# Weight casts behind the copies, matmuls on a constant at the start, and first weights loaded in two parts, in a two-layer encoder

## The chip, the cores and the metric

The kernel runs on one core of a Trainium2 chip. The metric is the device time of one execution in microseconds (us). The kernel before the change took 2218.75, 2219.17 and 2223.41 us in three runs; the median is 2219.17.

Five engines work side by side, each with its own queue of instructions that it takes in order: TensorE (PE), VectorE (DVE), ScalarE (ACT), GpSimd (POOL) and SyncE (SP). They wait for each other through semaphores. The loads are issued by SP; the transfers that add to what is already there are issued by POOL.

## The reference, cut to what matters

Two layers over 528 tokens (16 learned ones and 512 of the input) of 1024 channels, all in fp32. Each layer is a half-weighted SwiGLU feed-forward network (FFN), a mixer (gated linear attention and softmax attention, merged) and a second FFN.

```
def swiglu(x, w_gate, w_up, w_down):
    return (jax.nn.silu(x @ w_gate) * (x @ w_up)) @ w_down
...
    for l in range(DEPTH):
        h = h + 0.5 * swiglu(rmsnorm(h, norm_gains[l, 0]),
                             ffn_w_gate[l, 0], ffn_w_up[l, 0], ffn_w_down[l, 0])
        h = h + mixer(rmsnorm(h, norm_gains[l, 1]), w_in[l], ...)
        h = h + 0.5 * swiglu(rmsnorm(h, norm_gains[l, 2]),
                             ffn_w_gate[l, 1], ffn_w_up[l, 1], ffn_w_down[l, 1])
    return rmsnorm(h, final_norm)[:, N_META:]
```

The inner width of an FFN is 2816. The change touches only the four FFNs and the start of the first.

## The kernel before, in words

**Operands in two parts.** Every fp32 operand is split into a rounded part (hi, type fp32r) and the remainder (lo). A product of two operands is three matmuls, hi with hi, hi with lo and lo with hi. For a weight of 128x1024 the hi part is made by ACT in a cast (L244, about 1.05 us, into one of 4 buffers `whi`) and the remainder by DVE in a subtraction (L245, about 1.22 us, into one of 4 buffers `wlo`).

**Pairs and products.** The columns of gate and up are worked on in 11 pairs of 128-column blocks, in groups of 4, 4 and 3. For one pair the 2x2 block product with seven multiplications (Strassen and Winograd) is used: products 1, 2, 5, 6, 7, 4 and 3, each with its own combination of the weights and of the normed input. In this text (p,n) is product n of pair p, counted from pair 0 of its FFN. A product is 24 matmuls of 128x128 with 128x264 (L618) and needs one weight of 128x1024 in its hi and lo parts. In program order pair p+1's products 1 and 2 stand around pair p's 7 and 4. In the very first FFN, pair 0 is computed without the seven-product form, in two plain products (L575) with two weights each, so that TensorE can begin before all of the input is there; then come (1,1), (1,2), (1,6), (1,5), (2,1), (1,7), (2,2), (1,4), (1,3), (2,6), (2,5), (3,1).

**Weights.** SP loads a weight into one of three raw buffers. Four of the seven weights of a pair are sums and differences of blocks: `sums` (called from L250) has ACT negate a block (L192, tile `s`), and POOL issue transfers that add a block from memory or another tile to it (L197, `s<-win`, `w<-s`, `w<-win`, `s<-w`). One pass makes s3 and s2 for products 7 and 6, the other s1 and s4 for products 5 and 3. `use(j)` is called when product j is written out, and makes casts up to three or four products ahead.

**Banks.** A pair's products add up in three PSUM areas X, Y and Z. (p,6), (p,7) and (p,4) continue in X, where (p,1) began. ACT copies X out after products 1, 6 and 7 (`snapshot`, L629, tile `snap`), and the matmuls of the next product into that area wait for the copy. Y is freed by DVE's add of product 2 (L636), which reads the copy of product 1.

**What sets the order.** Instructions are written in one sequence, and a scheduler puts them on the engines by priorities; `tc.high_priority()` pulls an instruction forward, and `tc.issue_after(ins)` (through `after`) keeps one from being placed ahead of `ins`. Once placed, an engine's queue is fixed: an instruction that waits holds up all behind it. In the kernel before, the copies have ordinary priority, and one cast alone, that of the first FFN's (1,6), is held behind an instruction: `W.behind`, the last copy of the first two plain products (L584).

Of the kernel before, what the change touches and what calls it, by code (L numbers as in the profile page):

```python
# [17 lines left out]
P = 128  # L18
# [25 lines left out]
HELD = 4  # L44
SQUARES = {(1, "2"): (0, 1), (1, "6"): (2, 3), (1, "5"): (4, 5), (2, "1"): (6, 7)}
# [115 lines left out]

class Weights:
# [3 lines left out]
    def __init__(self, nc, after, raw, hi, lo, wts, win):  # L166
        self.nc, self.raw, self.hi_pool, self.lo_pool, self.wts, self.win = nc, raw, hi, lo, wts, win
        self.long = self.short = None
        self.loads = []
        for t, col in zip(PLAN, COLUMN):  # L170
            if t[0] == "op":
                self.loads.append(t[1:])
            elif col % SLAB == 0:
                self.loads.append(col // SLAB)
        self.at = {load: i for i, load in enumerate(self.loads)}
        self.made, self.fetched, self.got, self.summed, self.raws = 0, 0, {}, {}, {}
        self.pos, self.behind, self.after = 0, None, after
# [4 lines left out]
    def block(self, f, i, name, pool=None, tag="raw"):  # L182

        w = (pool or self.raw).tile([P, SLAB], F32, tag=tag, name=f"w{name}_{f[0]}{f[1]}_{i}")
        first = f + (i, name) == (0, 0, 0, "11")
        for a in np.split(np.arange(SLAB), 2 if first else 1):
            self.nc.sync.dma_start(w[:, a[0] : a[-1] + 1], self.dram(f, i, name)[:, a[0] : a[-1] + 1])
        return w

# [40 lines left out]
    def make(self, upto):  # L230
        nc = self.nc
        while self.made < min(upto, len(self.loads)):
# [8 lines left out]
            for a in np.split(np.arange(SLAB), 2 if s == 0 else 1):  # L241
                cs = slice(a[0], a[-1] + 1)
                with self.after(self.behind if load == ((0, 0), 1, "6") else None):
                    nc.scalar.copy(hi[:, cs], w[:, cs])  # L244
                nc.vector.tensor_tensor(lo[:, cs], w[:, cs], hi[:, cs].bitcast(F32), ALU.subtract)  # L245
# [6 lines left out]
    def use(self, j):  # L252
        self.make(j + AHEAD_MADE - (j < AHEAD_MADE))
# [25 lines left out]
def build(tc, ctx, xt, wts, win, par, w2, const, umask, out):  # L279
# [75 lines left out]
    S.activation(whole, eps.broadcast_to([P, P]), AF.Copy, scale=0.0, bias=1.0)  # L355
    b64, diag2 = ct[:, C_B64 : C_B64 + P], ct[:, C_DIAG : C_DIAG + P]
# [202 lines left out]
    def ffn(l, f, norm, done, following):  # L559
# [62 lines left out]
        def finished(p, product):  # L622
# [3 lines left out]
            def snapshot(name):  # L626
                t = slots["snap"].tile([P, T], F32, tag="snap", name=nm("snap"))[:, :n]
                st[name] = v2(t)
                S.copy(st[name], acc)  # L629
# [583 lines left out]
    bp = [block_pools()]  # L1213
    nc.sync.dma_start(h(1), xt[:, 1])
    first.whole(0)
# [89 lines left out]
```

## Time and profile before

| what | us |
|---|---|
| runs | 2218.75, 2219.17, 2223.41 (median 2219.17) |
| the profiled execution | 2222.56 |
| its span, first to last instruction | 2220.7 |
| TensorE (PE) busy | 2193.3 |
| VectorE (DVE) busy | 1515.2 |
| ScalarE (ACT) busy | 1218.6 |
| GpSimd (POOL) busy | 150.5 |
| first matmul starts | 6.59 |

All times in the profile count from the span's start. The four FFNs lie at about 6 to 385 us, 766 to 1100, 1129 to 1500 and 1866 to 2210; the mixers lie between. A row of a timeline gives the start, the length, the engine, the line, the operation, what is written and read, and a count, and in brackets the idle time ahead of it and what ended it. A row of the chain of waits gives start, length and what the end of the program hung on at that time. In the rows of windows the granted TensorE clock is 1.00 at full speed and 0.50 at half.

### The profile page before, as it was taken

What the parts mean: (1) busy time and instruction counts of PE and PEld (TensorE: products, weight loads), DVE (VectorE), ACT (ScalarE), POOL (GpSimd) and SP (SyncE); (2) the same over time, 40 slices, a digit from 0 to 9 for tenths busy, and PEclk for the clock granted to TensorE, in tenths of its full rate; (3) what the DMA queues carried; (4) which work ended last, traced back from release to release, by engine and by line L of the source; (5) the groups of instructions that cost most, each with busy time, mean ns of one, the idle gap of its engine ahead of it and who ended that gap; (6) DMA issues with size and microseconds to landing.
All of it is one profiled execution on the core that took longest, in us unless ns stands there. A gap on an engine that the chain in (4) does not pass through costs nothing.

```text
span 2220.7 us, 39865 instructions
## 1 busy us (share of the span) xinstructions
PE 2193.3 (99%) x16538; PEld 2094.3 (94%) x16538; DVE 1515.2 (68%) x2406; ACT 1218.6 (55%) x1824; POOL 150.5 (7%) x176
## 2 busy tenths in 40 slices
PE   8999999999999999999999999999999999999998
PEld 8999999999999999999999999999888888989897
DVE  7757567577876676565786575675889767756575
ACT  8535355455784574443575363554557837636354
POOL 1011000000000010101010110000000001101010
PEclk9999999999999999999999999999999999999999
DMA  8669563212113585867677685632211146968562
GB/s 258 182 175 231 142 152 110 77 48 68 48 39 126 140 218 143 202 171 176 170 174 191 171 215 142 157 110 77 67 67 48 48 133 158 240 152 223 152 168 67
DMA packets 87542, 312.85 MB, mean 141 GB/s; under 512 B 9664, under 2 KB 11840, under 8 KB 87360
## 3 DMA queue, kind: packets, MB, share of 16 engines
q1 hardware_dynamic: 60816, 217.67, 28.9%
q0 software_dynamic: 24768, 90.19, 22.9%
q8 instruction: 130, 2.13, 0.4%
q10 hardware_dynamic: 1776, 2.43, 0.4%
q14 instruction: 52, 0.43, 0.1%
HBM read 263.07 MB, written 2.10 MB: 119 GB/s over the span
## 4 chain that ended last, share of the span: by engine, by line
PE 88%; DVE 5%; ACT 4%; DMA 2%; issue 1%; DVEq 0%; SPq 0%; ACTq 0%; POOLq 0%
PE ss L618 38%; PE ss L409 26%; PE mm L409 13%; PE sm L409 2%; DVE wlo L245 1%; PE sm L1004 1%; DMA w<-win 1%; ACT whi L244 1%; PE ss L979 1%; ACT t L392 1%; PE sm L1020 1%; PE ss L980 1%; PE sm L1021 1%; PE ss L600 1%; PE ss L1190 0%
## 5 line engine op out<-in xcount | busy, mean ns | idle before, releaser
L618 PE MATMUL ss<-xc,whi 128*128 128x264 f32 (+1 forms) x4720 | 862.2, 284 | 4.3 <-ACT snap L629 4.1
L618 PEld LDWEIGHTS ss<-xc,whi 128*128 128x128 f32 x4720 | 732.7, 189 | 6.4 <-ACT snap L629 5.3
L618 PE MATMUL ss<-xc,wlo 128*128 128x264 f32 (+1 forms) x2360 | 670.0, 284 | 1.0 <-DVE wlo L245 1.0
L409 PE MATMUL ss<-g,whi 128*128 128x264 f32 (+1 forms) x2620 | 482.5, 300 | 0.0
L618 PEld LDWEIGHTS ss<-xc,wlo 128*128 128x128 f32 x2360 | 445.5, 189 | 1.6 <-DVE wlo L245 1.6
L409 PEld LDWEIGHTS ss<-g,whi 128*128 128x128 f32 x2620 | 380.8, 188 | 15.9
L409 PE MATMUL mm<-x,whi 128*128 128x264 f32 (+1 forms) x1712 | 384.3, 314 | 0.0
L244 ACT CAST whi<-w 128x1024 fp32r<-128x1024 f32 (+1 forms) x220 | 229.9, 1046 | 248.5 <-PE ss L409 113.4
L244 ACT CAST whi<-raw 128x1024 fp32r<-128x1024 f32 x190 | 199.2, 1048 | 278.3 <-PE ss L618 91.5
L245 DVE TENSOR_TENSOR wlo<-w,whi 128x1024 fp32r<-128x1024 f32 (+1 forms) x220 | 266.7, 1217 | 105.8 <-ACT whi L244 104.4
L409 PE MATMUL ss<-g,wlo 128*128 128x264 f32 (+1 forms) x1310 | 302.4, 300 | 0.0
L245 DVE TENSOR_TENSOR wlo<-raw,whi 128x1024 fp32r<-128x1024 f32 x190 | 232.0, 1221 | 93.9 <-ACT whi L244 89.8
L409 PEld LDWEIGHTS mm<-x,whi 128*128 128x128 f32 x1712 | 279.1, 188 | 15.9 <-DVE x L398 0.2
L409 PE MATMUL mm<-x,wlo 128*128 128x264 f32 (+1 forms) x856 | 265.3, 315 | 0.0
L409 PEld LDWEIGHTS ss<-g,wlo 128*128 128x128 f32 x1310 | 209.4, 188 | 8.1
L245 DVE TENSOR_TENSOR wlo<-s,whi 128x1024 fp32r<-128x1024 f32 x86 | 105.1, 1222 | 93.5 <-ACT whi L244 93.5
L244 ACT CAST whi<-s 128x1024 fp32r<-128x1024 f32 x86 | 90.3, 1051 | 142.6 <-PE ss L618 122.7
L409 PEld LDWEIGHTS mm<-x,wlo 128*128 128x128 f32 x856 | 159.6, 188 | 8.3
L192 ACT ACTIVATE s<-w 128x1024 f32<-128x1024 f32 x86 | 91.2, 1060 | 84.8 <-DMA w<-win 54.5
L546 DVE SCALAR_TENSOR_TENSOR t<-ss,rs 128x528 f32<-128x528 f32 (+1 forms) x64 | 44.3, 700 | 126.1 <-PE ss L409 126.0
L197 POOL DMA_DIRECT2D w<-win x43 | 37.7, 876 | 958.6 <-DVE wlo L245 396.7
L197 POOL DMA_DIRECT2D s<-win x43 | 39.9, 927 | 536.9 <-ACT s L192 536.9
(284 smaller groups left out, 2838.0 us busy)
## 6 DMA issues: line engine op xcount, KB each, us to landing
w<-win SPq DMA_DIRECT2D x218, 512.0 KB, 4.8
raw<-wts SPq DMA_DIRECT2D x190, 512.0 KB, 3.3
s<-win POOLq DMA_DIRECT2D x43, 512.0 KB, 7.0
w<-win POOLq DMA_DIRECT2D x43, 512.0 KB, 7.9
w<-s POOLq DMA_DIRECT2D x43, 512.0 KB, 5.4
s<-w POOLq DMA_DIRECT2D x43, 512.0 KB, 6.7
h<-xt SPq DMA_DIRECT2D x3, 528.0 KB, 6.9
out<-h SPq DMA_DIRECT2D x2, 512.0 KB, 2.9
```

What stands on the lines that cost most here:

```text
L192: self.nc.scalar.activation(t, w, AF.Copy, scale=-1.0)
L197: self.nc.gpsimd.dma_start(t, src, accum_op=ALU.add)
L244: nc.scalar.copy(hi[:, cs], w[:, cs])
L245: nc.vector.tensor_tensor(lo[:, cs], w[:, cs], hi[:, cs].bitcast(F32), ALU.subtract)
L392: prev_act[0] = S.activation(*args, **kw).ins
L409: TE.matmul(acc.half[i][:width], lhs, rhs[:, acc.spans[i]], start=first, stop=last)
L546: V.scalar_tensor_tensor(cut(dst[rows]), pv[rows], -0.5 * f, cut(rs[rows]), ALU.mult, ALU.mult)
L600: TE.matmul(acc[:, j], a[:, j, k], b[:, at], start=k == 0 and i == 0, stop=k == last and i == 2)
L618: TE.matmul(acc[:, j], a[:, j, k], b[:, at], start=bool(begin and k == 0 and i == 0), stop=k == len(x) - 1 and i == 2, skip_group_check=no ...
L979: TE.matmul(s[:n, i, :HF], lhs, kh[:, hs], start=True, stop=False)
L980: TE.matmul(s[:n, i, :HF], lhs, kl[:, hs], start=False, stop=True)
L1004: TE.transpose(tp[:, j * w + u * n : j * w + (u + 1) * n], pr[:n, (2 * c2 + j) * P : (2 * c2 + j + 1) * P], ident[:n, :n])
```

## The change

1. **Matmuls on a constant.** DVE fills a 128x512 tile with a constant, and TensorE runs ten matmuls on it into PSUM that nobody reads, ahead of the first product.
2. **First weights in two parts.** The first two weights ("11" and "12" of pair 0) are loaded in two parts: first the columns of the first of four row blocks (256 of 1024), later the rest (`finish_loads`). Their casts and remainders are made in the same two parts. SP's queue at the start is now: input chunk 0, head of "11", input chunk 1, head of "12", rest of "11", rest of "12", the other input chunks. Before: input chunks 0 and 1, "11" in two halves, "12", the other chunks.
3. **Casts behind the copies.** Each copy that frees a bank (`snapshot`) gets high priority and is stored in `W.behind`, and every FFN weight cast for gate and up is issued after the copy that was stored last when it is written.
4. **When casts are made.** `use(j)` makes casts up to j + 4 for j above 4, and up to 6 for the first five; before it was j + 3 below 4 and j + 4 from there on. The casts of (1,6) and (1,5) are so written at the use of (1,2) and not of (1,1).

```
+WARMING = 10
...
+PIECES = (slice(0, 1), slice(1, KC // 2))
+def by_pair(ap):
+    return ap.rearrange("p (w k m) -> p w k m", w=2, k=KC // 2)
...
     def block(self, f, i, name, pool=None, tag="raw"):
         w = (pool or self.raw).tile([P, SLAB], F32, tag=tag, name=f"w{name}_{f[0]}{f[1]}_{i}")
-        first = f + (i, name) == (0, 0, 0, "11")
-        for a in np.split(np.arange(SLAB), 2 if first else 1):
-            self.nc.sync.dma_start(w[:, a[0] : a[-1] + 1], self.dram(f, i, name)[:, a[0] : a[-1] + 1])
+        src = self.dram(f, i, name)
+        if f + (i,) == (0, 0, 0) and name in ("11", "12"):
+            head, tail = [(by_pair(w)[:, :, ks], by_pair(src)[:, :, ks]) for ks in PIECES]
+            self.nc.sync.dma_start(*head)
+            self.rest.append(tail)
+        else:
+            self.nc.sync.dma_start(w, src)
         return w
+    def finish_loads(self):
+        for t in self.rest:
+            self.nc.sync.dma_start(*t)
...
-            for a in np.split(np.arange(SLAB), 2 if s == 0 else 1):
-                cs = slice(a[0], a[-1] + 1)
-                with self.after(self.behind if load == ((0, 0), 1, "6") else None):
-                    nc.scalar.copy(hi[:, cs], w[:, cs])
-                nc.vector.tensor_tensor(lo[:, cs], w[:, cs], hi[:, cs].bitcast(F32), ALU.subtract)
+            for part in [[by_pair(t)[:, :, ks] for t in (hi, lo, w)] for ks in PIECES] if s < 2 else [(hi, lo, w)]:
+                with self.after(None if isinstance(load, int) else self.behind):
+                    nc.scalar.copy(part[0], part[2])
+                nc.vector.tensor_tensor(part[1], part[2], part[0].bitcast(F32), ALU.subtract)
...
     def use(self, j):
-        self.make(j + AHEAD_MADE - (j < AHEAD_MADE))
+        self.make(j + AHEAD_MADE if j > AHEAD_MADE else AHEAD_MADE + 2)
...
+    idle = slot("t", F32R)[:, :512]
+    V.tensor_copy(idle, eps.broadcast_to([P, 512]))
+    for _ in range(WARMING):
+        TE.matmul(pair()[:, 0], idle[:, :P], idle, start=True, stop=True)
...
             def snapshot(name):
                 t = slots["snap"].tile([P, T], F32, tag="snap", name=nm("snap"))[:, :n]
                 st[name] = v2(t)
-                S.copy(st[name], acc)
+                with tc.high_priority():
+                    W.behind = S.copy(st[name], acc).ins
...
+    W.fetch(1)
     nc.sync.dma_start(h(1), xt[:, 1])
+    W.fetch(2)
+    W.finish_loads()
     first.whole(0)
```

Three places show what moves on the engines. The lines of the change are numbered differently from those of before: L260 is the cast (L244 before), L261 the remainder (L245), L650 the copy (L629), L209 the negation (L192), L657 DVE's add of product 2 (L636), L638 the product's matmuls (L618), L440 the matmuls of the norm's totals (L420). Tile numbers differ too.

**ACT at the end of (1,2) in the first FFN**, before. whi_484 and whi_488 are the hi parts for (1,6) and (1,5), snap_516 is the copy of (1,1), t are squares for the norm.

```order
L455 ACTIVATE t_518<-h 128x528
L584 COPY c_378<-ss_382 128x528
L244 CAST whi_484<-w_00_1_220 128x1024
L244 CAST whi_488<-w_00_1_249 128x1024
L455 ACTIVATE t_520<-h 128x528
L629 COPY snap_516<-ss_483 128x528
L244 CAST whi_524<-w_00_2_383 128x1024
L455 ACTIVATE t_562<-h 128x528
```

And with the change (snap_533 is the copy, whi_541, whi_545 and whi_549 the three casts):

```order
L475 ACTIVATE t_587<-h 128x528
L475 ACTIVATE t_590<-h 128x528
L650 COPY snap_533<-ss_508 128x528
L260 CAST whi_541<-w_00_1_245 128x1024
L260 CAST whi_545<-w_00_1_274 128x1024
L260 CAST whi_549<-w_00_2_408 128x1024
L260 CAST whi_593<-s_00_1_242 128x1024
L475 ACTIVATE t_625<-h 128x528
```

The copy has moved from behind two casts to the front of them, and a third and a fourth cast follow directly. On DVE the three remainders wlo_542, wlo_546 and wlo_550 now stand in a row ahead of the add c_585 of (1,2):

```order
L261 TENSOR_TENSOR wlo_542<-w_00_1_245,whi_541 128x1024
L261 TENSOR_TENSOR wlo_546<-w_00_1_274,whi_545 128x1024
L261 TENSOR_TENSOR wlo_550<-w_00_2_408,whi_549 128x1024
L657 TENSOR_TENSOR c_585<-snap_533,ss_540 128x2x264
L261 TENSOR_TENSOR wlo_594<-s_00_1_242,whi_593 128x1024
```

Before, DVE had two remainders, an addition of squares, the third remainder and then this add. Earlier on ACT, the negation of pair 1's block 11 stood ahead of both copies of the first product (L584); now it stands behind the first of them and one activation.

**ACT from (2,1) to (1,4) in the first FFN**, before. snap_676 is the copy of (2,1), snap_706 that of (1,7), s_00_3_814 the negation for pair 3.

```order
L244 CAST whi_648<-w_00_1_572 128x1024
L415 CAST t_710<-t_518 128x528
L244 CAST whi_678<-s_00_1_252 128x1024
L629 COPY snap_676<-ss_647 128x528
L192 ACTIVATE s_00_3_814<-w_00_3_745 128x1024
L629 COPY snap_706<-ss_483 128x528
```

And with the change (snap_701 of (2,1), snap_731 of (1,7)):

```order
L260 CAST whi_673<-w_00_1_597 128x1024
L650 COPY snap_701<-ss_672 128x528
L260 CAST whi_703<-s_00_1_277 128x1024
L435 CAST t_735<-t_535 128x528
L209 ACTIVATE s_00_3_839<-w_00_3_770 128x1024
L650 COPY snap_731<-ss_508 128x528
```

The copy of (2,1) has changed places with the cast; the copy of (1,7) still stands behind the negation.

**ACT from (0,7) to (0,4) in the third FFN**, before. snap_13653 is the copy of (0,7), whi_13673 a cast of a weight made by transfers, rs the norm's factor.

```order
L244 CAST whi_13623<-w_10_1_13297 128x1024
L192 ACTIVATE s_10_2_13714<-w_10_2_13627 128x1024
L244 CAST whi_13673<-w_10_1_13398 128x1024
L433 ACTIVATE rs_13656<-ss_13661,eps 128x528
L629 COPY snap_13653<-ss_13393 128x528
L392 ACTIVATE rs_13656<-rs_13656 128x528
```

And with the change:

```order
L260 CAST whi_13648<-w_10_1_13322 128x1024
L209 ACTIVATE s_10_2_13739<-w_10_2_13652 128x1024
L650 COPY snap_13678<-ss_13418 128x528
L453 ACTIVATE rs_13681<-ss_13686,eps 128x528
L260 CAST whi_13698<-w_10_1_13423 128x1024
L412 ACTIVATE rs_13681<-rs_13681 128x528
```

The copy now stands ahead of the factor and of the cast. On PE, between the totals of the norm (L420, L440) and the first matmul of (0,4), 14 matmuls of (1,6) stood before; with the change there are 2, and the other 12 come later.

1 line of the change is left out of this document (added).

## The prediction

> **What bounds the kernel now.** I read the page's busy shares and groups, then PE's waits, then the chain of waits, and last the timelines of PE, ACT, DVE and POOL around each wait that the change can touch. First the page.
>
> ```profile
> span 2220.7 us, 39865 instructions
> PE 2193.3 (99%) x16538; PEld 2094.3 (94%) x16538; DVE 1515.2 (68%) x2406; ACT 1218.6 (55%) x1824; POOL 150.5 (7%) x176
> L618 PE MATMUL ss<-xc,whi 128*128 128x264 f32 (+1 forms) x4720 | 862.2, 284 | 4.3 <-ACT snap L629 4.1
> L244 ACT CAST whi<-raw 128x1024 fp32r<-128x1024 f32 x190 | 199.2, 1048 | 278.3 <-PE ss L618 91.5
> ```
>
> TensorE is busy for 99% of the span; only its idle time and its clock can change. The last row says that a cast usually idles until PE gives a buffer back, so most weights are ready well ahead. PE's waits that the edits name (total, times, longest):
>
> ```profile
> PE ss L575 <- ACT whi L244: 6.6, 1, 6.6
> PE ss L618 <- ACT snap L629: 4.1, 3, 1.9
> PE ss L618 <- DVE wlo L245: 1.0, 2, 0.5
> ```
>
> So 6.6 us before the first matmul, 4.1 us for copies that free a bank, 1.0 us for remainders. The profiled execution took 2222.56 us, 1.86 more than its span, and the median of the runs is 2219.17. The windows below explain that distance (stretch, length and PE's busy time with its instructions, then PEld, DVE, ACT, POOL; the granted clock stands ahead of the last two columns).
>
> ```profile
> 37.77:41.18 3.41, 1.61 (x14) 1.39 (x13) 3.33 (x4) 3.41 (x6) 1.37 (x2) 1.00 0.81 154
> 41.18:44.59 3.41, 3.41 (x18) 3.41 (x17) 3.31 (x5) 3.41 (x7) 0.00 (x0) 0.50 1.00 175
> 1150.52:1153.93 3.41, 1.51 (x13) 1.30 (x12) 1.72 (x2) 2.77 (x5) 0.02 (x1) 1.00 1.02 271
> 1153.93:1157.34 3.41, 3.41 (x18) 3.41 (x17) 1.97 (x4) 0.56 (x1) 0.00 (x0) 0.50 1.06 222
> ```
>
> Each stretch in which PE was busy for only 1.61 or 1.51 us is followed by one at clock 0.50, which costs half of 3.41 = 1.71 us. 2222.56 − 2 × 1.71 = 2219.14, the median: I take it that the faster runs had no slow stretch. A long stall is thus priced twice, once as idle time and once as a slow stretch, and the second part varies from run to run.
>
> The Trainium skill, "TensorE: Matmul & The Clock Gate", section "Part 1: The HAM clock gate (the "warmup" mystery)", gives the same free-running window of 3413 ns, but throttles only after a whole idle window. By that rule neither stretch above would have slowed, and removing the stalls would save 1.71 us less for each; the rows show that 1.8 us of idle time was enough, so I go by the rows.
>
> **Wait A, 38.0 to 39.8 us: product 6 of pair 1, written (1,6).** The chain, then ACT and PE:
>
> ```profile
> 18.37 0.95 ACT s L192
> 19.64 9.79 DMA s<-win
> 29.71 7.03 DMA w<-s
> 36.77 1.99 ACT L244 CAST whi<-w 128x1024 fp32r<-128x1024 f32 x2 [3.70 <-DMA w<-s]
> 38.67 0.64 ACT L455 ACTIVATE t<-h 128x528 f32<-128x528 f32 x1
> 39.21 0.58 ACT L629 COPY snap<-ss 128x528 f32<-128x528 f32 x1
> 37.76 0.28 PE L618 MATMUL ss<-xc,wlo 128*128 128x264 f32 x1
> 39.84 0.51 PE L618 MATMUL ss<-xc,whi 128*128 128x264 f32 x2 [1.80 <-ACT snap L629]
> 37.85 2.36 DVE L245 TENSOR_TENSOR wlo<-w,whi 128x1024 fp32r<-128x1024 f32 x2 [5.33 <-ACT whi L244]
> ```
>
> The copy of (1,1) stands on ACT behind two casts whose weight, a sum made by transfers, lands at 36.75. Part 3 puts the copy ahead, so the bank is free long before. But (1,6) itself needs that weight: its hi part at 36.77 + 1.05 = 37.82, its remainder at 37.85 + 1.22 = 39.07. A product is 24 matmuls:
>
> ```profile
> 273.82 52.70 PE ss L618 x432
> ```
>
> 52.70 / 432 = 0.122 us each, 2.93 a product. Two matmuls run at 37.8, the third at 39.09, and 22 more steps of 0.122 end at 41.77; before, at full clock, it ended at 39.84 + 2.93 = 42.77. Next, (1,5) needs the bank that DVE's add of (1,2) frees, which is now queued behind three remainders instead of standing after the third with others between: 37.85 + 3 × 1.14 = 41.27, and 0.70 for the add gives 41.97. So (1,5) starts at 42.0, a gain of 0.77, not 1.80: the stall goes over to the weight and to this add.
>
> **The start (parts 1 and 2) is covered.** Two rows of PE while it is cold, the row of ACT that makes the second quarter of the operands, and the queues' rows of the windows 19.7 to 24.5 and 24.5 to 29.5 us (packets, MB, share):
>
> ```profile
> 7.20 0.42 PE L575 MATMUL ss<-xc,whi 128*128 128x264 f32 x1
> 7.42 0.42 PE L575 MATMUL ss<-g,whi 128*128 128x264 f32 x1
> 9.40 0.50 ACT L476 ACTIVATE xc<-h,par 128x264 fp32r<-128x264 f32 x1
> q1 hardware_dynamic: 409, 1.49, 89.5%
> q0 software_dynamic: 208, 0.79, 85.1%
> ```
>
> A cold matmul of 264 columns steps by 0.22 us, so ten of 512 take 10 × 0.22 × 512 / 264 = 4.3 us and fit, from about 1.6 to 5.9, into the 6.6 us of idle time; were the constant late, they would delay the first product by at most their overhang, below 1 us. PE is then at full clock earlier, but it can't go past the operands that ACT makes from 9.40 on: I put the first product's end at 19.1 (estimate: some 0.6 us by the earlier start of the weights, some 0.6 by the clock), against 20.3 now. Nothing of it reaches the end, since (1,6) waits for the chain above: PE comes to (1,6) at about 36.8 instead of 38.04 and waits there. What is on that chain is the negation (row 18.37): it now stands behind the first copy of the first product and one more activation, 1.04 us later. Between 19.7 and 24.5 us only the queue of the loads moved (409 packets); the sum's transfer, issued at 19.64, shows its first packets after 24.5 (208 up to 29.5). Issued 1.04 us later it still stands ready before 24.5, so this costs nothing (bounds 0 and 1.04; I take 0). SP's two more issues move the same bytes ahead of that.
>
> **Wait B, 53.8 us, (1,4).** The chain:
>
> ```profile
> 50.32 1.06 ACT whi L244
> 51.41 1.24 DVE wlo L245
> 52.66 1.06 ACT s L192
> 53.72 0.50 ACT snap L629
> 54.26 0.51 PE L618 MATMUL ss<-xc,whi 128*128 128x264 f32 x2 [0.44 <-ACT snap L629]
> ```
>
> The copy of (1,7) stays behind the negation, which stays behind this remainder; the copy of (2,1) now goes ahead of the cast, 0.49 more in the chain. (2,1) ends 0.77 earlier, so PE resumes 0.28 earlier than before at full clock: 52.37 against 52.65, or 1.89 earlier than the profiled 54.26, whose 1.71 was the slow stretch. What is late next is the weight of (3,1):
>
> ```profile
> 48.07 0.87 POOL L197 DMA_DIRECT2D w<-win  x1 [1.65 <-DVE wlo L245]
> 58.12 1.06 ACT L244 CAST whi<-w 128x1024 fp32r<-128x1024 f32 x1 [1.15 <-DMA w<-win]
> 64.81 1.22 DVE L245 TENSOR_TENSOR wlo<-w,whi 128x1024 fp32r<-128x1024 f32 x1
> 66.31 0.28 PE L618 MATMUL ss<-xc,wlo 128*128 128x264 f32 x1
> ```
>
> Its remainder is ready at 66.03, 0.28 before PE uses it. It hangs on the transfer issued at 48.07 and landing at 58.05 (ahead of the cast at 58.12). That issue waited 1.65 for a remainder which comes earlier now, so it can go at most 1.65 earlier. ACT stands idle for 1.15 before the cast, and the activations between 58 and 64 wait for PE. So (3,1) starts between 0.26 (PE again slowed) and 1.89 us (everything follows) earlier than profiled; I take the middle, 1.05.
>
> **Wait C, third FFN, 1151.4 us, (0,4).** ACT, then PE:
>
> ```profile
> 1148.21 1.06 ACT L192 ACTIVATE s<-w 128x1024 f32<-128x1024 f32 x1 [0.34 <-DVE wlo L245]
> 1151.13 1.05 ACT L244 CAST whi<-w 128x1024 fp32r<-128x1024 f32 x1 [1.86 <-DMA w<-win]
> 1152.68 0.59 ACT L629 COPY snap<-ss 128x528 f32<-128x528 f32 x1
> 1149.06 0.65 PE L420 MATMUL ss<-t,whole 128*128 128x264 f32 x4
> 1153.32 0.52 PE L618 MATMUL ss<-xc,whi 128*128 128x264 f32 x2 [1.90 <-ACT snap L629]
> ```
>
> (0,7) had ended when the totals of row 1149.06 began, and ACT was idle from 1149.27 to 1151.13, waiting for a weight with the copy queued behind it. Ahead of the cast the copy runs at 1149.2 to 1149.8. PE does the totals and two matmuls until 1149.8 and goes on, with 0.1 us of wait: −1.8. The 12 matmuls that filled the time before come later, in the place of others, at no cost. The late weight, cast at 1151.13, is wanted some 5 us after. With the stall the slow stretch goes: −1.71.
>
> **Elsewhere**, part 3 makes ACT do the copy about 0.95 us earlier and the cast 0.49 later, through all pairs, and part 4 only makes the casts of (1,6) and (1,5) come at the use of (1,2) instead of (1,1), so that they stand behind the copy of (1,1), as counted in A. The casts' idle time before, ended by PE (278.3 us over 190 for one group, 1.5 each), covers 0.49; the two remainder waits of 0.5 us stay. Without that cover 0.49 per copy would be due, which I do not expect.
>
> **Sum** against the profiled time: 2222.56 − 1.05 − 1.8 − 1.71 = 2218.0 (2217.1 to 2218.8 by the bounds of A and B). Against the median, without slow stretches: there (3,1) would wait for its weight, and the gain is 0.8 instead of 1.05: 2219.17 − 0.8 − 1.8 = 2216.6. A run after the change will be one or the other; I take the middle, **2217.3**.
>
> **Rivals.** (1) *The moved negation comes through.* If the loads and the sum's transfer share the engines in turn, the 1.04 us pass to (1,6), which then ends at 42.8 as before; A and B together give 0.3 and the sums 2218.75 and 2217.4, so about 2218.1. Against it stand the two queue rows, in which one queue had all the time. The Trainium skill ("DMA: Bandwidth & Descriptors", section "SWDGE vs HWDGE vs iDMA") says that an engine goes round between the two kinds of queues; by that this rival would hold, but the row of 409 to none disagrees. (2) *Slower: more slow stretches.* PE comes to (1,6) 1.2 us earlier with the weight unmoved; it idles from 36.8 to 37.8, 38.1 to 39.1 and 41.8 to 42.0, 2.2 us against 1.80. Spread over two stretches, each has some 1.1 us idle, and if that is enough, both that follow are slow: 2219.17 − 1.8 + 2 × 1.71 = 2220.8. It decides if 1.1 us of idle time in a stretch suffices; the rows show only that 1.8 does. (3) *All three stalls and both stretches go*: 2222.56 − 1.80 − 0.44 − 1.90 − 3.42 = 2215.0, or 2213.8 if the 1.2 us of the start come through as well. It needs the weight of (1,6) to land over 1 us earlier, and nothing in the change moves its transfers forward. (4) *The change does nothing*: some other waiting instruction keeps the copies late: 2219.2.
>
> **Chances.** Forecast 0.55 (own range 2215.5 to 2219.5), rivals 0.13, 0.11, 0.17, 0.04. What a measurement can tell from no change is about 0.2%, 4.4 us: faster means below 2214.7, slower above 2223.6. Below lie half of rival 3 (0.08) and the low tail of the rest (0.10): 0.18. Above lie a part of rival 2 and a weight that loses its slack somewhere in 44 pairs: 0.07. Same 0.75. The range, 2213.5 to 2221.5, takes in rivals 2 and 3.
>
> **What would show it.** After the change PE's wait for a copy at (0,4) of the third FFN should be below 0.2 us, and no clock of 0.50 near 1154. (1,6) should wait for the cast or its remainder, (1,5) for DVE's add, and PE should resume (1,4) by a copy near 52.4 (54 if slowed). The sum's first packets should still come after 24 us. Wrong it would be by new waits for remainders of 0.4 us or more in the steady pairs, by two slow stretches in the first FFN, or by a (1,6) that starts before 37.

## The result and the profile after

The changed kernel took 2226.46 us (median of 8 runs, 2224.08 to 2231.54) against 2219.85 for the kernel before (8 runs, 2218.75 to 2225.18): a ratio of 1.0029, 95% interval 1.0016 to 1.0041. It is 6.6 us slower, where 2217.3 was forecast with a range up to 2221.5.

The profiled execution of the change took 2231.54 us, the longest of its eight. Its page, the lines that answer to those shown of before:

```profile
span 2229.6 us, 39823 instructions
PE 2201.3 (99%) x16548; PEld 2100.2 (94%) x16548; DVE 1518.6 (68%) x2408; ACT 1221.5 (55%) x1825; POOL 150.8 (7%) x176
L638 PE MATMUL ss<-xc,whi 128*128 128x264 f32 (+1 forms) x4720 | 861.7, 284 | 4.5 <-DVE t L458 3.5
L260 ACT CAST whi<-raw 128x1024 fp32r<-128x1024 f32 x190 | 199.8, 1051 | 279.3 <-PE ss L638 92.4
```

The span grew by 8.9 us and PE's busy time by 8.0 (with the ten matmuls on the constant in it). The products' matmuls (L638) take what they took before, and the casts idle for the same 279 us until PE frees a buffer. So nothing is lost in the steady part; PE ran slower, or waited, at a few places. Of its waits, those on which the change bears (total, times, longest):

```profile
PE ss L638 <- DVE t L458: 3.5, 1, 3.5
PE ss L595 <- ACT xc L496: 2.6, 1, 2.6
PE ss L620 <- DVE h L571: 1.9, 1, 1.9
PE ss L638 <- DVE wlo L261: 1.7, 3, 0.8
PE ss L638 <- ACT snap L650: 0.4, 1, 0.4
```

The 4.1 us for copies are down to 0.4, and the 6.6 us before the first matmul are filled by those on the constant (which themselves wait 1.4 us for it). Three new waits stand there instead: 2.6 for the second quarter of the operands, 3.5 for the norm's factor, and 1.9 in front of the third FFN. Around each of them the windows of the change (columns as in the prediction):

```profile
10.31:13.72 3.41, 1.64 (x11) 1.50 (x12) 3.17 (x7) 3.38 (x9) 0.00 (x0) 1.00 1.03 420
13.72:17.14 3.42, 3.42 (x18) 3.42 (x18) 3.42 (x10) 3.42 (x8) 0.00 (x0) 0.50 1.00 402
58.10:61.51 3.41, 1.41 (x12) 1.19 (x10) 0.51 (x1) 1.59 (x2) 0.96 (x2) 1.00 0.64 135
61.51:64.93 3.42, 1.95 (x9) 1.95 (x10) 3.35 (x5) 2.93 (x4) 0.82 (x1) 0.50 0.99 175
64.93:68.34 3.41, 3.41 (x17) 3.41 (x17) 3.41 (x8) 2.56 (x5) 0.00 (x0) 0.50 0.98 198
1136.71:1140.12 3.41, 1.48 (x10) 1.14 (x10) 2.42 (x5) 2.06 (x4) 0.00 (x0) 1.00 0.98 264
1140.12:1143.54 3.42, 3.42 (x18) 3.42 (x17) 3.37 (x8) 3.19 (x7) 0.00 (x0) 0.50 0.01 2
```

Each wait ends in a stretch at clock 0.50 or is followed by one, the one at the factor by two: a wait is paid for twice, as the prediction had it of the old waits. The chain of waits through the first FFN says how the second wait comes about (start, length, what; the short rows of issuing are left out):

```profile
3.78 5.89 DMA w<-win
9.69 0.83 ACT whi L260
...
11.62 0.42 ACT xc L496
12.08 9.40 PE ss L595 x60
21.50 0.60 ACT c L604
22.10 0.64 ACT t L504
22.74 0.96 ACT s L209
24.02 7.52 DMA s<-win
31.82 8.13 DMA w<-s
...
41.09 7.86 DMA s<-win
49.30 10.60 DMA w<-s
59.92 1.04 ACT whi L260
60.97 0.55 ACT rs L412
61.54 0.65 ACT t L457
62.22 0.72 DVE t L458
```

The rest of the second weight lands at 9.67. Its cast stands on ACT ahead of the second quarter of the operands, PE waits for those, and its product ends late; so the copy (21.50) and the negation behind it (22.74; 18.37 before) are late, and with them all the sums that transfers make, one after the other. The last, a weight of pair 2, lands at 59.90 (54.20 before). Its cast stands on ACT between the two steps of the norm's factor, and PE waits for the factor.

**Where the time is.** To compare traces beyond one wait I count matmuls from the end: the start of the matmul that has so many behind it in the record, in us. Both kernels were profiled a second time, for a reason given below.

| matmuls behind it | place | before | before, 2nd | change | change, 2nd |
|---|---|---|---|---|---|
| 16,442 | the 96th of the first FFN | 20.18 | 22.74 | 22.64 | 23.87 |
| 16,178 | ahead of the factor | 56.68 | 56.31 | 58.13 | 57.59 |
| 16,038 | behind the factor | 73.75 | 75.55 | 81.34 | 79.09 |
| 13,538 | end of the first FFN | 378.23 | 380.03 | 385.81 | 383.56 |
| 12,000 | in the first mixer | 570.15 | 573.51 | 579.43 | 577.17 |
| 7,500 | ahead of the third FFN | 1124.91 | 1128.08 | 1134.10 | 1131.71 |
| 7,000 | in its first group | 1190.84 | 1190.68 | 1199.16 | 1196.64 |
| 50 | end | 2203.24 | 2202.98 | 2211.75 | 2209.03 |

The first pair of executions is 8.98 us apart, the second (2222.21 and 2228.74) 6.53, close to the medians. The second pair's distance grows by 1.3 us up to the factor, by 2.3 across it, by 0.1 up to 1128 and by 2.3 at the start of the third FFN; 0.44 lie behind the last of these marks, from there to the span's end: 17.9 us in the five traces with loads in two parts, 17.4 to 17.5 in the other eleven. So part 2 has this cost as well; its cause was not followed up. The first pair's grows by 1.5, 6.1 and 1.6, then falls by 0.9. Between the places both kernels keep the same pace: from 73 to 378 us they take 304.5, and from 1191 on 1012.3 to 1012.6, in all four.

### The profile page after: what moved, and what is told of

The parts are those of the page before. It is cut to its first block, busy times and chain, and to the rows that moved or that the text cites. A ratio compares the mean times of both kernels' runs of the same rounds, so it can differ in the third digit from the quotient of the medians.

```text
span 2229.6 us, 39823 instructions
## 1 busy us (share of the span) xinstructions
PE 2201.3 (99%) x16548; PEld 2100.2 (94%) x16548; DVE 1518.6 (68%) x2408; ACT 1221.5 (55%) x1825; POOL 150.8 (7%) x176
## 4 chain that ended last, share of the span: by engine, by line
PE 89%; DVE 5%; ACT 3%; DMA 2%; issue 1%; SPq 0%; DVEq 0%; POOL 0%; ACTq 0%; POOLq 0%
PE ss L638 38%; PE ss L429 26%; PE mm L429 14%; PE sm L429 2%; PE sm L1025 1%; DVE wlo L261 1%; PE ss L620 1%; DMA w<-s 1%; PE ss L1000 1%; DMA s<-win 1%; ACT t L412 1%; PE sm L1041 1%; PE ss L1001 1%; ACT whi L260 1%; PE sm L1042 1%
## 5 line engine op out<-in xcount | busy, mean ns | idle before, releaser
L638 PE MATMUL ss<-xc,whi 128*128 128x264 f32 (+1 forms) x4720 | 861.7, 284 | 4.5 <-DVE t L458 3.5
L638 PEld LDWEIGHTS ss<-xc,whi 128*128 128x128 f32 x4720 | 732.3, 189 | 6.6 <-DVE t L458 3.7
L638 PE MATMUL ss<-xc,wlo 128*128 128x264 f32 (+1 forms) x2360 | 669.7, 284 | 1.7 <-DVE wlo L261 1.7
L638 PEld LDWEIGHTS ss<-xc,wlo 128*128 128x128 f32 x2360 | 445.1, 189 | 2.5 <-DVE wlo L261 2.4
L260 ACT CAST whi<-raw 128x1024 fp32r<-128x1024 f32 x190 | 199.8, 1051 | 279.3 <-PE ss L638 92.4
L260 ACT CAST whi<-w 128x1024 fp32r<-128x1024 f32 (+1 forms) x221 | 230.6, 1045 | 196.5 <-PE ss L429 116.0
L261 DVE TENSOR_TENSOR wlo<-w,whi 128x1024 fp32r<-128x1024 f32 (+1 forms) x221 | 267.0, 1213 | 93.3 <-ACT whi L260 90.7
L261 DVE TENSOR_TENSOR wlo<-raw,whi 128x1024 fp32r<-128x1024 f32 x190 | 232.2, 1222 | 93.9 <-ACT whi L260 89.8
L261 DVE TENSOR_TENSOR wlo<-s,whi 128x1024 fp32r<-128x1024 f32 x86 | 105.2, 1223 | 108.8 <-ACT whi L260 108.8
L260 ACT CAST whi<-s 128x1024 fp32r<-128x1024 f32 x86 | 90.6, 1053 | 102.7 <-PE ss L638 83.7
L209 ACT ACTIVATE s<-w 128x1024 f32<-128x1024 f32 x86 | 91.3, 1061 | 89.8 <-DMA w<-win 52.3
L650 ACT COPY snap<-ss 128x528 f32<-128x528 f32 (+1 forms) x129 | 76.2, 590 | 93.0 <-PE ss L638 91.9
```

The source lines that it names most:

```text
L209: self.nc.scalar.activation(t, w, AF.Copy, scale=-1.0)
L260: nc.scalar.copy(part[0], part[2])
L261: nc.vector.tensor_tensor(part[1], part[2], part[0].bitcast(F32), ALU.subtract)
L638: TE.matmul(acc[:, j], a[:, j, k], b[:, at], start=bool(begin and k == 0 and i == 0), stop=k == len(x) - 1 and i == 2, skip_group_check=no ...
L650: W.behind = S.copy(st[name], acc).ins
```

## The experiments

The quoted expectations use single letters for theories. S: the loss is made at the start. O: the casts behind the copies hold other work up. X: wait C was an accident of one execution. R: the transfers of part rows are slow. N: the late negation makes the sums late. M: the sums' transfers wait for the loads anyway. B: a bank exchanged in the third FFN. F: the cast ahead of the factor. Another letter is explained where it stands. Ratios are to the kernel before, run beside it, with 95% intervals; before's median lay between 2218.30 and 2219.06 in these sessions.

### The parts apart

Four kernels: the order alone (parts 3 and 4), the change without the split loads (1, 3 and 4), the split alone (2), the constant alone (1). What is taken out of the change for parts 1 and 2:

```
-    idle = slot("t", F32R)[:, :512]
-    V.tensor_copy(idle, eps.broadcast_to([P, 512]))
-    for _ in range(WARMING):
-        TE.matmul(pair()[:, 0], idle[:, :P], idle, start=True, stop=True)
...
-        if f + (i,) == (0, 0, 0) and name in ("11", "12"):
...
+        first = f + (i, name) == (0, 0, 0, "11")
+        for a in np.split(np.arange(SLAB), 2 if first else 1):
+            self.nc.sync.dma_start(w[:, a[0] : a[-1] + 1], self.dram(f, i, name)[:, a[0] : a[-1] + 1])
```

and for parts 3 and 4:

```
-                with self.after(None if isinstance(load, int) else self.behind):
+                with self.after(self.behind if load == ((0, 0), 1, "6") else None):
...
-        self.make(j + AHEAD_MADE if j > AHEAD_MADE else AHEAD_MADE + 2)
+        self.make(j + AHEAD_MADE - (j < AHEAD_MADE))
...
-                with tc.high_priority():
-                    W.behind = S.copy(st[name], acc).ins
+                S.copy(st[name], acc)
```

> Parts 3 and 4 alone (casts behind copies), loads and start as before. Theory S (the loss is made at the start: the rests of the first weights land late, and with them the operands of the second quarter, the negation and the chain of sums): no loss here, wait C gone, but the first product of the third FFN waits 1.9 us for its bank in its place, so 2217.5 to 2220.5, ratio 0.999 to 1.0005. Theory O (casts behind copies hold other work up): 2224 to 2227, ratio above 1.002.

> The change without part 2 (loads as before). Theory S: the negation stands behind the first copy, but that copy comes at about 19.9 us, so the sums are late by about 1 us or less: 2218 to 2221.5. Theory O: 2224 to 2227. If the constant matmuls were at fault: also 2224 to 2227, but then the run with parts 3 and 4 alone is near 2219.

> Part 2 alone (first two weights in two parts), the rest as before. Theory S: PE waits 1 to 2.6 us ahead of the second quarter of the first product, the negation ends near 23 us, and the loss shows here: 2223 to 2227, ratio 1.0015 to 1.004. Theory O: no loss, 2218.5 to 2220.5.

> Part 1 alone (ten matmuls on a constant). Theory S: the negation stands behind the first copy, about 1 us later, and the rest is as before: 2219 to 2221, ratio 0.9995 to 1.001. Theory O: 2218.5 to 2220.5. Both expect the first product at full clock by about 7 us and at most 1 us earlier at its end.

| kernel | median us | ratio |
|---|---|---|
| order alone (3, 4) | 2220.84 | 1.0009 [1.0000, 1.0018] |
| without the split (1, 3, 4) | 2222.42 | 1.0019 [1.0011, 1.0028] |
| split alone (2) | 2223.10 | 1.0019 [1.0010, 1.0027] |
| constant alone (1) | 2219.65 | 1.0004 [0.9995, 1.0013] |

No part gains. The split loses, and so does the order together with the constant. The order alone loses at the edge of its interval, and the constant alone can't be told from nothing. S put the order alone at a ratio up to 1.0005 and O above 1.002; it came between them, so neither S nor O alone is the cause.

### The two kernels again

The same two kernels, unchanged, for a second trace each; no edit.

> The kernel before, once more, for a second execution's trace. Theory X (wait C of the third FFN, 1.90 us and the slow stretch behind it, was an accident of the one execution profiled: a transfer that landed late): no wait for a copy at (0,4) in this one, wait A there again (1.5 to 3 us), 2217 to 2221. Rival: wait C belongs to this order of instructions and shows again with 1.5 to 2 us.

> The change once more, for a second execution's trace, since the one profiled was the slowest of its eight. Theory N (late sums): the first product ends near 22.6 us again and POOL's first issue is near 24, in every execution; how far the long wait near 60 us goes varies with the transfers (0 to 3.5 us), 2223 to 2229. Rival: the first product's end itself varies by over 1 us from one execution to the next.

The kernel before, second execution, PE's waits:

```profile
PE ss L575 <- ACT whi L244: 7.3, 2, 6.5
PE ss L618 <- DVE wlo L245: 1.9, 3, 0.9
PE ss L618 <- ACT snap L629: 1.3, 2, 1.1
PE ss L600 <- DVE h L551: 0.2, 1, 0.2
```

The 1.80 us of wait A and the 1.90 of wait C, each with a slow stretch in the prediction, are not in this trace, though every engine has the same instructions in the same order; X expected wait A again, and 2217 to 2221 us. The waits for copies are 1.3 us, the longest of 1.1 at 52.8, and remainders cost 1.9 instead of 1.0. X holds for C: in the seven traces whose order there is that of before it is 1.90 once, 1.05 once (part 1 with the edit of the negation, below) and under 1 us in five. Wait A is more than an accident: without part 3 it is 1.80 us in before, 3.00 in part 1 alone, 2.07 in part 2 alone, 3.20 in part 2 with whole loads (below), and under 0.5 us where PE comes late or the sum early. In before's second trace PE's matmuls kept the spacing of the cold clock until 15.2 us instead of 10.5, so it came to (1,6) later than the weight. The second trace of the change has the three new waits again, of 3.5, 2.6 and 1.9 us: they belong to the change. Their sizes vary: its 96th matmul starts 1.2 us later than in the first trace and POOL's first transfer goes out at 25.25 instead of 24.02, as the rival had it.

### Whole loads at the start

Part 2 with each first weight loaded in one transfer; casts and remainders still in two parts.

```
-            head, tail = [(by_pair(w)[:, :, ks], by_pair(src)[:, :, ks]) for ks in PIECES]
-            self.nc.sync.dma_start(*head)
-            self.rest.append(tail)
+            self.nc.sync.dma_start(w, src)
```

> Part 2 alone as before, but each of the two first weights is loaded in one transfer, in the same place of the queue; the casts stay in two parts. Theory R (rows of 512 and 1536 bytes move slowly, so the rests land late): DMA moves over 330 GB/s between 3 and 8 us again, PE waits under 0.7 us ahead of the second quarter, 2218.5 to 2221, ratio under 1.0011. Rival Q (the casts in parts and the place of the negation cost the time, not the rows): 2222 to 2224, ratio near 1.0019 as with part 2 alone.

It took 2222.02 us, ratio 1.0013 [1.0004, 1.0021]. The windows from 3 to 8 us say what the split does to the transfers (last columns: clock, share of the DMA engines' time, GB/s). The kernel before:

```profile
3.00:8.00 5.00, 1.41 (x6) 1.41 (x7) 3.31 (x8) 3.79 (x8) 0.00 (x0) 1.00 0.99 357
```

The change:

```profile
3.00:8.00 5.00, 5.00 (x21) 3.93 (x20) 2.47 (x7) 2.98 (x7) 0.00 (x0) 1.00 0.89 238
```

Part 2 alone:

```profile
3.00:8.00 5.00, 2.88 (x11) 2.54 (x12) 2.55 (x7) 3.08 (x7) 0.00 (x0) 1.00 0.90 231
```

And this kernel, with whole loads:

```profile
3.00:8.00 5.00, 2.57 (x10) 2.26 (x10) 3.35 (x7) 3.57 (x8) 0.00 (x0) 1.00 1.01 342
```

In the split a row of the first two weights is 512 or 1536 bytes; the rows of the input that pass in the same time are whole in all four. The DMA engines are busy for 0.89 of the time and move a third less. With whole loads the rate is back, and PE's wait for the second quarter, 2.47 us in part 2 alone and 2.58 in the change, is gone; a cast is waited for a little earlier, for 0.47. R holds for the transfers and this wait, not for its time (2218.5 to 2221). The Trainium skill ("DMA: Bandwidth & Descriptors", section "Why small descriptors are slow (HBM only)") gives a fixed overhead of some 3 cycles for each packet of 32-byte beats; an estimate from it is 3 on 16 cycles for 512 bytes and 3 on 48 for 1536, 6 on 64 or about 9% over the weight. The rows show the direction, but a third, so this overhead is not all of it. The median moved by only 1.1 us, within the intervals: in this kernel the sum's first transfer still goes out at 22.40 instead of 19.64, and PE, which comes earlier, waits 3.20 us at (1,6) for the copy behind the casts, wait A again.

### The negation first

The negation of pair 1's block 11 is pulled ahead of the copies of the first product: in the change, in part 2 with whole loads (the kernel above), and in part 1 alone.

```
-        self.nc.scalar.activation(t, w, AF.Copy, scale=-1.0)
+        with self.tc.high_priority() if f + (i, name) == (0, 0, 1, "s3") else nullcontext():
+            self.nc.scalar.activation(t, w, AF.Copy, scale=-1.0)
```

> The change, with the negation of pair 1 placed ahead of the first product's copies again. Theory N (the sums start late because the negation waits behind a copy for PE): POOL's first issue at 21 to 22 us instead of 24.0, the weight of (1,6) lands by 38.8 instead of 39.95, the long wait near 60 us shrinks below 2 us, 2221.5 to 2224, ratio 1.0012 to 1.0024. Rival M (the sums' transfers wait for the loads, whenever they are issued): no gain, 2224 to 2227, ratio 1.0025 to 1.004.

> Whole first loads in the new order of the queue, casts in two parts, and the negation of pair 1 ahead of the first product's copies. Theory N: what was left of the loss with whole loads (1.0013) was the negation: 2218 to 2220.5, ratio 0.9993 to 1.0006, the wait at (1,6) 1 us or more shorter than 3.20. Rival: the casts in parts or the order of the queue cost the rest, 2221 to 2223, ratio 1.001 to 1.0017.

> The constant matmuls alone, and the negation of pair 1 ahead of the first copy again. Theory N: 0.5 to 1.5 us less than with the constant matmuls alone (1.0004): 2217.5 to 2219.5, ratio 0.9990 to 1.0001. Rival M (the sums wait for the loads anyway): 2219 to 2221, ratio 1.0002 to 1.0007.

The change with it took 2222.66 us, 1.0017 [1.0008, 1.0026]; part 2 with whole loads 2219.22, 1.0003 [0.9994, 1.0012]; part 1 alone 2219.70, 1.0005 [0.9996, 1.0014]. N expected a gain of part 1 too, and that failed. The intervals with and without the edit overlap; the traces tell more. PE's wait of 3.20 us at (1,6) is gone from part 2 with whole loads, and that for the norm's factor from the change. POOL's rows show the first sum: s<-win and w<-s are its transfers, each issued when the one ahead has landed, and the issue of s<-w stands right behind the landing of the sum. The change:

```profile
24.02 1.01 POOL L214 DMA_DIRECT2D s<-win  x1 [23.57 <-ACT s L209]
31.82 0.87 POOL L214 DMA_DIRECT2D w<-s  x1 [5.39 <-DMA s<-win]
40.56 0.89 POOL L214 DMA_DIRECT2D s<-w  x1 [7.87 <-DMA w<-s]
```

The kernel before, second execution:

```profile
20.36 1.01 POOL L197 DMA_DIRECT2D s<-win  x1 [19.92 <-ACT s L192]
29.78 0.86 POOL L197 DMA_DIRECT2D w<-s  x1 [6.56 <-DMA s<-win]
37.60 0.89 POOL L197 DMA_DIRECT2D s<-w  x1 [6.96 <-DMA w<-s]
```

The same rows of the other traces in which that issue waited for the sum (the last kernels of the table come below):

| kernel | first transfer issued | next issue, behind the landing of the sum |
|---|---|---|
| 2 with whole loads and the negation first | 19.39 | 35.60 |
| all mended, with the cast behind the factor | 19.39 | 37.11 |
| all mended but one | 19.46 | 37.49 |
| before | 19.64 | 37.35 |
| without the split | 21.16 | 37.21 |
| 1 alone | 21.27 | 38.04 |
| 2 with whole loads | 22.40 | 38.78 |
| the change, with the cast behind the factor | 23.63 | 40.21 |
| split alone | 24.91 | 40.96 |

Up to 21.3 us the issue moves nothing that stands out of the spread (35.6 to 38.7, the last in part 1 with the negation first, issued at 20.82); the loads stand ahead of the first transfer, as M and the prediction said. At 22.40 the sum is at the edge of this spread, and from 23.6 on it comes later, in the change by 3 us. So N holds for the split, and for part 1 there was little to gain: the edit moved the issue by 0.45 us only.

### The banks turned

In the trace of the order alone PE waits in front of the third FFN:

```profile
PE ss L609 <- DVE h L560: 1.5, 1, 1.5
```

With part 3 the last two down products of the second FFN take each other's PSUM areas, so that the third FFN's first product goes into the one that DVE's last add of h frees (0.2 us of wait in the kernel before, 1.9 in the change). This kernel is parts 3 and 4 with these two areas turned back:

```
             other = (sum(GROUPS[: g + 1]) - 1) % 2 == 0
+            if (l, f, g) == (0, 1, len(GROUPS) - 1):
+                other = not other
```

> Parts 3 and 4 alone, and in the last group of the second FFN the areas of the down products are turned round, so that the first product of the third FFN begins in one that is free early. Theory B (the 1.49 us wait there comes of the bank that the order of copies gave it): that wait is under 0.3 us and 1.2 us are won against parts 3 and 4 alone: 2218.5 to 2220.5, ratio 1.0 to 1.0009. Rival: something else late there, then a wait of 1 us or more stays and the time is 2220 to 2222.

It took 2220.43 us, 1.0003 [0.9995, 1.0012]. The wait at the third FFN is gone. A smaller one comes before it, where a down product waits for a cast near 1088 us:

```profile
PE ss L418 <- ACT whi L253: 1.1, 1, 1.1
```

From 7,500 to 7,000 matmuls before the end it takes 61.18 us, the order alone 62.93, the change 65.06. B holds for that wait, 1.75 us there without a slow stretch and 3.9 with one. But the new wait stands in each of the three traces with the areas turned and in no other, and the way from 12,000 to 7,500 takes 1.4 us more here than in the order alone (556.4 against 555.0). Near the end (50 matmuls behind it) the two are level, at 2201.11 and 2201.03: the 1.2 us were not won, and the medians don't separate the two kernels.

### All mended but one

The change with whole loads, the negation first and the areas turned: the three edits above together.

> All four parts of the change, with three things mended: the first loads whole, the negation first, and the down products' areas turned round in the last group of the second FFN. Theories R, N and B together: 2218 to 2220.5, ratio 0.999 to 1.0008, no wait over 1 us ahead of the second quarter, near 60 us or at the start of the third FFN. If the casts behind the copies cost time of their own (theory O): 2221 to 2223, ratio above 1.001.

It took 2222.00 us, 1.0011 [1.0003, 1.0020]: still slower, in the range of O. PE's longest wait:

```profile
PE ss L638 <- DVE t L458: 2.7, 1, 2.7
```

And the last transfer of pair 2's sum in the chain of waits (start, length):

```profile
46.05 9.95 DMA w<-s
```

PE comes to the factor 3.1 us earlier than in the change (16,178 matmuls before the end at 55.02 instead of 58.13), the sum lands at 56.0, and ACT stands at its cast until then. What the start gained is given back at the factor.

### The cast behind the factor

That cast is issued behind the last activation of the norm's factor, in the change alone and in the mended kernel.

```
-        S.activation(u, y, AF.Square, scale=n ** -0.5)
+        W.factor = S.activation(u, y, AF.Square, scale=n ** -0.5).ins
...
                     rsqrt_of(ms, rs, True, D)
+            if self.gc == G_NORM:
+                W.behind = W.factor
             return rs
```

> The change, with the cast of pair 2's sum (product 6) placed behind the three steps of the norm's factor instead of between the first and the second. Theory F (that cast waits for a late sum and holds up the factor, and with it a bank that PE needs near 60 us): the wait there falls from 2.6 to 3.5 us to under 0.5 us, and the ratio from 1.0029 to 1.0010 to 1.0022 (2221 to 2224). Rival: (2,6) itself then waits for the sum as long, and the time stays at 1.0025 to 1.0035.

> The mended change (whole first loads, negation first, areas turned round), with the cast of pair 2's sum behind the norm's factor as well. Theory F: the 2.7 us wait near 57 us and the slow stretch behind it go, 2217 to 2220, ratio 0.999 to 1.0005 against 1.0011. Rival: another wait of 1 us or more in the first FFN takes its place (at (2,6) or (3,1)), ratio 1.0006 to 1.0015.

The change with it: 2221.95 us, 1.0016 [1.0007, 1.0025]. The mended kernel with it: 2218.55, 1.0003 [0.9995, 1.0012]. In the mended kernel the sum of pair 2 comes no earlier, as the chain of waits has it:

```profile
45.58 10.35 DMA w<-s
```

But the wait for the factor is gone. PE's waits there:

```profile
PE ss L640 <- DVE wlo L260: 2.3, 4, 0.8
PE ss L640 <- ACT whi L259: 0.5, 1, 0.5
```

A cast is still waited for, for 0.5 us.

The 140 matmuls across the factor (16,178 to 16,038 from the end) put all traces side by side:

| kernels | us | the cast waits on ACT for the sum |
|---|---|---|
| before; 1 alone, and with the negation first; 2 alone, with whole loads, and with both; the change with the negation first | 17.1 | not at all |
| order alone; with areas turned | 19.0 | 0.4, 0.5 |
| before, 2nd | 19.2 | not at all |
| without the split; all mended but one | 21.3, 21.6 | 2.7, 2.9 |
| the change, two executions | 21.5, 23.2 | 2.8, 3.7 |
| the cast behind the factor, two kernels | 17.8, 17.9 | moved |

Where the cast waits 2.7 us or more, the stretch takes 4.2 to 6.1 us more than the shortest, and moving one cast takes that away: F holds. In the order alone, with areas turned and in before's second trace PE waits for the factor 0.33 us at most; the 1.9 to 2.1 us more are there mostly a wait in (3,1), for a weight whose transfer landed late (see wait B below). The change with the negation first has no such wait, since its start still makes PE come to the factor at 57.59; all mended but one, PE is there at 55.02 and waits. Where part 3 is left out, PE has waited for the same transfers already at (1,6), in front of the copy.

With the start, the cast and the areas all mended, the change is where the kernel before is (1.0003). With the cast left as it is the median is 3.3 us above before, with the start and the areas left 3.7. None of the kernels beat before.

## Why the prediction was wrong

**Wait A: right.** The order did what the prediction said. The change has no wait for a copy over 0.4 us; its weight at (1,6) lands at 39.95, 3.2 us later than before, and PE waits only 0.58 and 0.75 there, for the cast and a remainder, as "(1,6) should wait for the cast or its remainder" said (the wait of (1,5) for DVE's add did not come). With a weight so late (1,6) starts 1.2 us later than before all the same. In the order alone it starts 1.1 us earlier (38.75), and PE is at the mark ahead of the factor at 55.35, 1.3 and 1.0 earlier than in before's two traces.

**"The start (parts 1 and 2) is covered": wrong.** Two steps in it failed. "SP's two more issues move the same bytes ahead of that": the same bytes, but at 231 to 238 GB/s instead of 339 to 357, so that the weights' rests were cast at 8.33 and 9.69, ahead of operands that the prediction took to come from 9.40 on, and came from 11.52 on. The first product's end, put at 19.1 against 20.3 before, is 22.8 in the change. And "Issued 1.04 us later it still stands ready before 24.5, so this costs nothing" kept its mechanism and lost its size: without the split the issue did come 1.5 us later at no cost (21.16, and the next issue at 37.21), but in the change the negation started 4.36 later (22.63 against 18.27), its transfer went out at 24.02, where the cover has ended. The working took the shift from the order (one copy and one activation) and left out that this copy waits for PE, whose own time it had just put at an estimate.

**Wait B, −1.05: wrong in both places.** "What is late next is the weight of (3,1)" came true in the order alone, but the term did not. PE resumes (1,4) there at 52.93, 1.33 us earlier than before's first trace, and then waits 0.93 us in (3,1) for the remainder: the matmul that reads it starts at 66.68, 0.37 later than before's 66.31. The step that failed is that the transfer would go and land earlier: it was issued 0.66 earlier (47.41) and landed 0.6 later (58.64 instead of 58.05). The chain of waits of the order alone:

```profile
47.41 11.23 DMA w<-win
58.72 1.06 ACT whi L253
```

There was no room behind it either: the activations between 58 and 64 do not wait for PE, as the prediction has it, but in before (the first at 61.09) for DVE, which has come to them straight from this weight's remainder. With the constant and the order together, what came first was another weight, the one of pair 2 that transfers make. In the trace of before its cast already stands between two steps of the factor, and has little room (ACT, before):

```profile
54.11 0.71 ACT L433 ACTIVATE rs<-ss,eps 128x528 f32<-128x528 f32 x1
54.70 1.05 ACT L244 CAST whi<-w 128x1024 fp32r<-128x1024 f32 x1
55.64 0.65 ACT L392 ACTIVATE rs<-rs 128x528 f32<-128x528 f32 x1
```

The sum landed at 54.20 and the cast began at 54.70, 0.50 us of slack in a chain that PE waits for. The prediction followed the weight whose wait the trace showed, and not this one, which had none yet. The factor comes earlier with parts 3 and 4 (its first step at 52.78 in the order alone) while the sum hardly does, so the slack is gone even where the start is not late: PE waits 0.23 us for the factor in the order alone and 2.4 in the kernel without the split, where PE is earlier still and the sum's last transfer takes 10.0 us instead of 8.6. In the change the sum is another 5.7 us late on top.

**Wait C, −1.8 and −1.71: wrong in what it was subtracted from.** Part 3 removes the wait for the copy at (0,4), but five of the seven traces of before's order have no wait of 1 us there to remove. Both terms, and with them "2222.56 − 2 × 1.71 = 2219.14, the median", took one execution's accident for the kernel's own: the second execution took 2222.21 us without A and C. And part 3 put a wait of 1.3 to 1.9 us in its neighbourhood that the prediction does not have, by the areas that the scheduler gave to two down products.

**"Elsewhere", no cost: right.** From 1191 us on the four traces take 1012.3 to 1012.6.

**The rivals.** The first, that the moved negation comes through, happened with four times its shift. The second, more slow stretches, happened with its price of 1.71 each, but at other places and after longer waits than its 1.1 us; behind the first product no idle stretch of that length was followed by a slow one. What the runs add up to is a mechanism that no rival had: an earlier PE runs into a cast that waits for a chain of transfers, and the part that was to help the start makes this chain later.

Still open is how much each mechanism is worth in the median. Not every pair of the three was tried, and the intervals of the single ones overlap; that mending the start, the cast and the areas together brings the time back is shown, the shares are read from single traces, and by these the areas won little on balance.

## What to carry to other kernels

A wait in one profile is not yet the kernel's own: take a second profile before pricing its removal, above all when it hangs on a transfer. When an edit lets an engine arrive earlier, list every instruction on the path that now waits for something that does not move, and look at the slack of each, also of those that show no wait yet: here one cast with 0.50 us of slack, placed between two steps of a norm, gave back what a better start had won. And when a load is split, compare the bytes of a row before and after, not only the bytes in all.

## What the runs showed of the chip that was not expected

- **Part rows.** From 3 to 8 us the loads moved at 231 and 238 GB/s in the two traces shown with rows of 512 and 1536 bytes among them, and at 342 and 357 in the two without such rows.
- **The clock.** A wait of PE of 1.80 us or more was followed by a stretch at half clock each time, in ten traces; waits of 1.05 to 1.60 us behind the first product were not, in nine. A slow stretch with 1.95 us of work in it (61.51 to 64.93) was followed by another. The Trainium skill ("TensorE: Matmul & The Clock Gate", section "Part 1: The HAM clock gate (the "warmup" mystery)") throttles after a whole idle window; the windows shown throttle with PE busy for 1.41 to 1.64 of 3.41 us.
- **A slow stretch that comes and goes.** In the first mixer, from 13,538 to 12,000 matmuls before the end, the traces take either 191.9 to 192.0 us (8 of 16) or 193.4 to 193.6 (the other 8), with no relation to the edits that I can see: both sides have kernels with and without each part, and before has one trace on each. Each of the slower eight has one stretch of 3.41 us at clock 0.50 there, which starts between 564 and 570 us. PE's record shows no wait ahead of it (in before's second trace busy for 3.41 of 3.41 us, from 561.38 on), but 18 to 20 of the 28 or 29 matmuls that start in the 3.41 us ahead write only 2 or 16 columns. So a busy PE alone does not keep the clock; that the narrow matmuls are the cause is not shown.
- **The transfers that add.** The one that makes the sum of pair 2 took 8.6 us in before's first trace and 6.6 in its second, and 10.0 to 10.6 in six of the seven traces with parts 1, 3 and 4 together, with 1.71, 1.40 and 2.06 to 2.12 MB of loads passing meanwhile. The seventh, the change with the negation first, has 6.7 us and 1.15 MB. Whether more loads make the transfer longer, or more loads pass because it takes longer, is not shown.
